# Attention's background work: order of the weight pieces, one bank for the block MLP, query splits one head at a time

## The chip, the core and the metric

The kernel runs on one core of one Trainium2 chip. The metric is the device time of one execution in microseconds (us); three runs of the kernel before gave a median of 1116.23 us (1115.17 to 1118.41). Times below are in us unless marked ns. PE is the tensor engine (PEld its weight load), DVE the vector engine, ACT the scalar engine, POOL GpSimd, and SP the engine whose queue issues most DMAs.

## The reference, cut to what matters

Two layers over 512 tokens of width 1024. The first is a short convolution with an MLP; then one shared key/value side is made; the second layer is native sparse attention with an MLP. The change touches only the attention.

```python
kv = (h @ w_kv).reshape(B, S, 6, 4, 64)            # 6 parts, 4 groups, 64 wide
k_raw, v_raw, k_sel, v_sel, k_win, v_win = (kv[:, :, i] for i in range(6))
k_cmp = compress_blocks(k_raw, cmp_pe_k, phi_k_w1, phi_k_w2)   # blocks of 32, stride 16 -> 31 tokens
v_cmp = compress_blocks(v_raw, cmp_pe_v, phi_v_w1, phi_v_w2)   # silu(flat @ w1) @ w2
q, gates = split(h2 @ w_qg)                        # 16 heads: 4 groups of 4
# per block of 128 queries, with a relative-position bias on all logits:
o = g0 * softmax(q k_cmp) v_cmp + g1 * softmax(q k_sel) v_sel + g2 * softmax(q k_win) v_win
x = x + o @ w_o
```

With 512 tokens the top-16 selection takes every causal block, and the window covers all tokens, so the selected and the windowed branch are both full causal attention with their own keys and values.

## The kernel before, in words

Every product of float32 values is made from float16 halves: a value is split into a high part `hi` and the remainder `lo`, and a product is three matmuls, hi x hi, hi x lo and lo x hi (`mm3`, L355 to L358). Weights come as 512 KB pieces in a fixed order (`pieces`, L74 to L132): `load_piece` issues the DMA on SP's queue (L150 to L173), with up to three pieces staged, `convert_piece` (L175 to L210) scales and splits one piece, on ACT (`whi`, L202) and DVE (`wlo`, L203), and `next_piece` (L213) hands the next one to its user, in the order of the list. `ahead_fine` (L707) converts up to two pieces ahead of use, 512 columns at a time, between the matmuls of whoever runs it.

Attention starts with a lead-in (L919): keys and values of the selected and windowed branches, queries of group 0, gates. Then comes a loop over 96 **items** (L1157). An item is one of

- `Full` (L971), 88 of them: logits of one group, one block of 128 queries and one branch against all earlier keys. An item has 512, 384, 256 or 128 columns a head, with one, two or four heads, so that it stays within 512 columns.
- `Cmp` (L1044), 8 of them: the compressed branch for two groups and one block of queries.

An item goes through five steps, which the loop hands out to different turns (`lead`, L1155). `st0`: logits on PE into PSUM bank tag "b" (two banks; L991 and L992, for `Cmp` L1061 and L1062), then DVE adds the bias and takes the row minimum (`at_s`, `at_m`, L999; three buffers of `at_s`), and ACT takes the exponential (`at_p`, L1001). `st1`, two turns later: PE transposes (bank "c", L1007), ACT takes the high half (`at_ph`, L1010). `st2`, three turns later: DVE takes the low half (`at_pl`, L1013). `st3`, four turns later: PE multiplies with the values (bank "d", L1026 to L1028; `Cmp` bank "e", L1098 to L1100); after the last head DVE scales by gate and row sum (`o_t`, L944), and POOL adds into `o` (L946, L949). `st4`, six turns later: PE transposes `o` (L960), and ACT and DVE split it into `big` (L377, L379), the operand of the output projection.

Beside the items runs a **background**, a chain of generators (L1140) that are pulled one step at a time. Each step tells its weight (0.65 for three matmuls of 512 columns, 0.42 for six of phi's of 155 columns); the loop adds a credit for each item (L1167: 1.03 up to item 43, then 0.78, 0.8 and 0.65) and pulls steps until the credit is used up. The parts stand one behind the other: `raw(0)`, `queries(1)`, `phi(0)`, `raw(1)`, `queries(2)`, `phi(1)`, `queries(3)`, then, once groups 0 and 1 are finished ("o1"), the output projection `out_proj(0)`. If an item needs something that is not yet done (`need`, L979 and L1050), the loop pulls the background until it is.

The background's parts, as far as the change touches them:

- `gated_pair` (L689): the projection of two 128-column blocks into two banks of tag "a" (there are two), in two pieces of weights. Used by `raw` and `queries`.
- `raw` (L786): the raw keys or values. DVE scales out of the "a" banks into `at_s` in another order of tokens (L797), ACT and DVE split it into `kr_hl` (one buffer; L377, L379), and twelve DMAs on SP's queue copy it into `big` (L803 to L805), the operand of phi.
- `phi` (L811): the block MLP. Four pieces of w1, each 24 matmuls of 155 columns from `big` into two banks of tag "a" (L823); then bias, tanh and split (L832 to L838, L381), and the second product into bank "e".
- `queries(g)` (L768): DVE scales the two "a" banks into `at_s` (L681), ACT copies each of the four heads to float16 (`Q`, L778, 64 partitions x 512), and POOL takes each remainder (L779). All four heads follow each other at once; three buffers of `Q`.

A scheduler places the instructions of each engine by their order in the source and by what they wait for; the order that results can be read from the built program.

## Time and profile before

| what | value |
|---|---|
| median of three runs | 1116.23 us (1115.17 to 1118.41) |
| the profiled execution | 1115.42 us |
| its span, first to last instruction | 1113.6 us |
| granted clock of PE | 0.998 of full |
| attention's items, first and last logits | about 549.8 and 757.0 us into the span |

The profile is of one execution. Its page gives the busy time of each engine, the chain of work that ended last, and the costliest groups; the trace behind it answers for single stretches and instructions. In a row "a<-b,c" is an instruction's output and inputs by their names in the program, "128x512" partitions by elements, and "[0.52 <-DVE at_s L797]" an idle time of the engine right before the instruction, with the instruction that ended it. "L797" is a line of the kernel before.

### The profile page before, as it was taken

What the parts mean: (1) busy time and instruction counts of PE and PEld (TensorE: products, weight loads), DVE (VectorE), ACT (ScalarE), POOL (GpSimd) and SP (SyncE); (2) the same over time, 40 slices, a digit from 0 to 9 for tenths busy, and PEclk for the clock granted to TensorE, in tenths of its full rate; (3) what the DMA queues carried; (4) which work ended last, traced back from release to release, by engine and by line L of the source; (5) the groups of instructions that cost most, each with busy time, mean ns of one, the idle gap of its engine ahead of it and who ended that gap; (6) DMA issues with size and microseconds to landing.
All of it is one profiled execution on the core that took longest, in us unless ns stands there. A gap on an engine that the chain in (4) does not pass through costs nothing.

```text
span 1113.6 us, 20039 instructions
## 1 busy us (share of the span) xinstructions
PE 1091.4 (98%) x7960; PEld 693.9 (62%) x7960; DVE 869.5 (78%) x1627; ACT 571.7 (51%) x922; POOL 58.5 (5%) x75
## 2 busy tenths in 40 slices
PE   9999999999999999999999999899999999999996
PEld 4444444446885448875767676675444788445895
DVE  5755466987988667969588889997998698875776
ACT  4532244545433444437578787875755433352352
POOL 1000000000000000000102021212000000000020
PEclk9999999999999999999999999999999999999999
DMA  6433335543333333303434242112653333330321
GB/s 214 132 97 95 114 95 151 152 119 108 114 115 115 99 109 99 111 18 119 122 98 132 66 128 63 39 40 64 184 158 106 98 118 108 114 95 1 96 77 76
DMA packets 149708, 115.74 MB, mean 104 GB/s; under 512 B 8700, under 2 KB 146640, under 8 KB 149616
## 3 DMA queue, kind: packets, MB, share of 16 engines
q1 hardware_dynamic: 146624, 108.88, 32.5%
q10 hardware_dynamic: 2608, 4.97, 1.5%
q8 instruction: 62, 1.02, 0.4%
q0 software_dynamic: 384, 0.63, 0.2%
q14 instruction: 30, 0.25, 0.1%
HBM read 110.22 MB, written 2.14 MB: 101 GB/s over the span
## 4 chain that ended last, share of the span: by engine, by line
PE 86%; DVE 7%; ACT 3%; issue 2%; POOL 1%; DMA 0%; DVEq 0%; ACTq 0%; SPq 0%
PE c L576 8%; PE a L576 8%; PE a L357 6%; PE a L356 6%; PE a L358 6%; PE b L576 6%; PE c L357 6%; PE c L358 6%; PE c L356 6%; PE b L358 6%; PE b L357 5%; PE b L356 5%; PE d L576 4%; PE e L576 2%; PE c L1007 2%
## 5 line engine op out<-in xcount | busy, mean ns | idle before, releaser
L202 ACT ACTIVATE whi<-wst 128x1024 f16<-128x1024 f32 (+3 forms) x172 | 144.3, 854 | 185.3 <-PE b L357 65.5
L203 DVE SCALAR_TENSOR_TENSOR wlo<-wst,whi 128x1024 f16<-128x1024 f32 (+3 forms) x172 | 170.1, 998 | 42.0 <-ACT whi L202 41.5
L576 PEld LDWEIGHTS <-whi 128*128 128x128 f16 x1792 | 175.3, 98 | 20.7
L358 PEld LDWEIGHTS <-wlo 128*128 128x128 f16 x1024 | 100.2, 98 | 111.7 <-DVE wlo L203 0.5
L356 PEld LDWEIGHTS <-whi 128*128 128x128 f16 x1024 | 100.3, 98 | 109.5 <-issue 2.5
L357 PEld LDWEIGHTS <-whi 128*128 128x128 f16 x1024 | 100.2, 98 | 108.4 <-issue 2.8
L189 ACT ACTIVATE whi<-wst 128x1792 f16<-128x1792 f32 x64 | 108.5, 1700 | 109.7 <-DVE wst L187 41.5
L190 DVE SCALAR_TENSOR_TENSOR wlo<-wst,whi 128x1792 f16<-128x1792 f32 x64 | 129.3, 2023 | 15.8 <-ACT whi L189 15.8
L187 DVE TENSOR_TENSOR wst<-wst 128x256 f32<-128x256 f32 x256 | 96.1, 428 | 19.6 <-DMA wst<-mlp_w_dram 18.3
L527 DVE TENSOR_TENSOR rl<-ml_z,rh 128x1792 f16<-128x1792 f32 x32 | 64.8, 2026 | 44.7 <-ACT rh L526 44.7
L576 PEld LDWEIGHTS <-wlo 128*128 128x128 f16 x896 | 87.7, 98 | 10.7 <-issue 0.2
L526 ACT ACTIVATE rh<-ml_z 128x1792 f16<-128x1792 f32 x32 | 54.3, 1696 | 57.3 <-DVE ml_z L525 57.3
L1001 ACT ACTIVATE at_p<-at_s,at_m 128x384 f32<-128x384 f32 (+3 forms) x128 | 70.8, 554 | 21.4 <-DVE at_m L999 20.5
L357 PE MATMUL b<-xsl,whi 128*128 128x512 f16 x208 | 78.9, 379 | 0.0
L358 PE MATMUL b<-xsh,wlo 128*128 128x512 f16 x208 | 78.9, 379 | 0.0
L356 PE MATMUL b<-xsh,whi 128*128 128x512 f16 x208 | 78.8, 379 | 0.0
L357 PE MATMUL c<-xsl,whi 128*128 128x512 f16 x192 | 72.8, 379 | 0.0
L356 PE MATMUL c<-xsh,whi 128*128 128x512 f16 x192 | 72.8, 379 | 0.0
L358 PE MATMUL c<-xsh,wlo 128*128 128x512 f16 x192 | 72.8, 379 | 0.0
L576 PE MATMUL c<-rh,whi 128*128 128x256 f16 x256 | 69.8, 273 | 0.0
L576 PE MATMUL c<-rl,whi 128*128 128x256 f16 x256 | 69.8, 273 | 0.0
L576 PE MATMUL c<-rh,wlo 128*128 128x256 f16 x256 | 69.8, 273 | 0.0
(318 smaller groups left out, 2549.9 us busy)
## 6 DMA issues: line engine op xcount, KB each, us to landing
wst<-mlp_w_dram SPq DMA_DIRECT2D x256, 256.0 KB, 3.4
wst<-a_w_in_dram SPq DMA_DIRECT2D x18, 512.0 KB, 3.6
wst<-w_kv_dram SPq DMA_DIRECT2D x12, 512.0 KB, 3.6
T<-ext_d ACTq DMA_DIRECT2D x4, 1056.0 KB, 6.1
wst<-a_w_out_dram SPq DMA_DIRECT2D x8, 512.0 KB, 3.5
wst<-b_w_qg_dram SPq DMA_DIRECT2D x8, 512.0 KB, 3.8
wst<-b_w_o_dram SPq DMA_DIRECT2D x8, 512.0 KB, 3.4
wst<-a_w_in_dram SPq DMA_DIRECT2D x7, 384.0 KB, 4.9
```

The lines of the kernel that those rows point to most:

```text
L187: DVE.tensor_tensor(b[:, :, o], b[:, :, x], b[:, :, y], op=e)
L189: ACT.activation(hi, b[:, :, 1:], AF.Copy, scale=sc)
L190: DVE.scalar_tensor_tensor(lo, b[:, :, 1:], sc, hi, op0=OP.mult, op1=OP.subtract)
L202: ACT.activation(hi[:, s:e], w, AF.Copy, scale=sc)
L203: DVE.scalar_tensor_tensor(lo[:, s:e], w, sc, hi[:, s:e], op0=OP.mult, op1=OP.subtract)
L356: PE.matmul(ps, w[0], xs[0], start=start, stop=False)
L357: PE.matmul(ps, w[0], xs[1], start=False, stop=False)
L358: return PE.matmul(ps, w[1], xs[0], start=False, stop=stop)
L526: ACT.activation(rh[0][:, p], z[:, 1:8], AF.Copy)
L527: DVE.tensor_tensor(rh[1][:, p], z[:, 1:8], rh[0][:, p], op=OP.subtract)
L576: PE.matmul(acc7[i], wl if n == 1 else wh, xl if n == 2 else xh, stop=c == 7 and n == 2, start=c == 0 and n == 0 and not other, skip_group ...
L1001: ACT.activation(self.p[:, w], lg[:, w], AF.Exp, bias=mn[:, j:j + 1], scale=-1.0, accum_out=l[:, br * 4 + h:br * 4 + h + 1])
```

## The change

- Pieces: the four pieces of phi_k_w1 and the two pieces of raw(1)'s weights (w_kv from column 256) now alternate: one, one, two, one, one.
- `phi` accumulates both halves in one bank, of tag "e" (columns 0 to 154 and 155 to 309), instead of two of tag "a"; only the first matmul of the first half opens the bank.
- The background runs `phi(0)` and `raw(1)` in turn, a step of each (`in_turn`).
- The generator that converts ahead is kept in one place (`fine`), and is finished before the next piece is handed out.
- `queries` scales into a tile of its own, `q_t`, instead of `at_s`. The four head splits go into a list (`later`), from which the loop takes one per item, or as many as an item needs. An item needs the last of its own heads ("q1.3"), not the whole group's.
- The compressed items of groups 0 and 1 stand behind the 4th, 6th, 8th and 10th item of group 2 (places 48, 51, 54, 57) instead of the 10th to 13th (54, 56, 58, 60).
- The credit is 1.17 up to item 46 and 0.65 after.

```diff
-    block(phi_k_w1, 0, SW, 0, 16)
+    for k in (0, 8):
+        block(phi_k_w1, 0, SW, k, 4)
+        cols(w_kv, 256, 256, SW, k // 2, 4)
+        block(phi_k_w1, 0, SW, k + 4, 4)
     cols(phi_k_w2, 0, 64, SW, 0, 2)
-    block(w_kv, 256)
...
         def ahead_fine():
-            while pos["cv"] < min(pos["use"] + AHEAD, len(pieces)):
-                yield from convert_piece(512)
+            drain(fine[0])
+            def convert():
+                while pos["cv"] < min(pos["use"] + AHEAD, len(pieces)):
+                    yield from convert_piece(512)
+            fine[0] = convert()
+            return fine[0]
...
             q = ap.tile([128, 4, S], F16, name="Q", bufs=3)
+            t = ap.tile([128, 2, S], F32, name="q_t", bufs=1)
+            Qs[g] = q
+            def head(h):
+                m, s = h // 2, h % 2
+                r, o = slice(64 * s, 64 * s + 64), slice(64 - 64 * s, 128 - 64 * s)
+                ACT.activation(q[r, h], t[r, m], AF.Copy)
+                POOL.tensor_tensor(q[o, h], t[r, m], q[r, h], op=OP.subtract)
+                done.add(f"q{g}.{h}")
             for m in range(2):
-                t = scaled(po[m], rbq)
-                for s in range(2):
-                    h, r = 2 * m + s, slice(64 * s, 64 * s + 64)
-                    o = slice(64 - 64 * s, 128 - 64 * s)
-                    ACT.activation(q[r, h], t[r], AF.Copy)
-                    POOL.tensor_tensor(q[o, h], t[r], q[r, h], op=OP.subtract)
-                yield
-            Qs[g] = q
+                DVE.tensor_tensor(t[:, m], po[m], rbq, op=OP.mult)
+            for h in range(4):
+                if lead_in[0]:
+                    head(h)
+                else:
+                    later.append(lambda h=h: head(h))
+            yield
...
-            ph = [bank("a"), bank("a")]
+            pb = bank("e")
+            ph = [pb[:, 0:155], pb[:, 155:310]]
...
-                        mm3(o, [...], rhs, cc == 0, cc == 15)
+                        mm3(o, [...], rhs, cc == 0 and m == 0, cc == 15, skip_group_check=m == 1)
...
+        def in_turn(*gens):
+            gens = list(gens)
+            while gens:
+                for k in list(gens):
+                    u = next(k, "end")
+                    if u == "end":
+                        gens.remove(k)
+                    else:
+                        yield u
...
-        items += mixed(full(2, (2, 3, 0, 1)), {9 + qb: Cmp(0, qb) for qb in range(4)})
+        items += mixed(full(2, (2, 3, 0, 1)), {3 + 2 * qb: Cmp(0, qb) for qb in range(4)})
...
             yield from raw(0)
-            yield from marked("q1", queries(1))
-            yield from phi(0)
-            yield from raw(1)
-            yield from marked("q2", queries(2))
+            yield from queries(1)
+            yield from in_turn(phi(0), raw(1))
+            yield from queries(2)
             yield from marked("cmp", phi(1))
-            yield from marked("q3", queries(3))
+            yield from queries(3)
...
                     while k not in done:
-                        if next(bg, "end") in ("wait", "end"):
+                        if later:
+                            later.pop(0)()
+                        elif next(bg, "end") in ("wait", "end"):
                             raise RuntimeError(k)
                 at_item.get(i, lambda: None)()
                 items[i].st0()
...
+                if later:
+                    later.pop(0)()
-            credit += 1.03 if i < 44 else 0.78 if i < 53 else 0.8 if i < 66 else 0.65
+            credit += 1.17 if i < 47 else 0.65
```

More of the change, by code (lines that the diff above doesn't have):

```diff
@@ L144, in body @@
     staged, ready = {}, {}
+    fine = [iter(())]
     pos = {"dma": 0, "cv": 0, "use": 0}
@@ L216, in next_piece @@
         pos["use"] += 1
+        drain(fine[0])
         while i not in ready:
-            for _ in convert_piece():
-                pass
+            drain(convert_piece())
         return ready.pop(i)
@@ L353, in rstd, with mm3 @@
             self.r = rstd_of(p[:, 0:4])
-    def mm3(ps, w, xs, start, stop):
-        PE.matmul(ps, w[0], xs[0], start=start, stop=False)
-        PE.matmul(ps, w[0], xs[1], start=False, stop=False)
-        return PE.matmul(ps, w[1], xs[0], start=False, stop=stop)
+    def mm3(ps, w, xs, start, stop, **k):
+        PE.matmul(ps, w[0], xs[0], start=start, stop=False, **k)
+        PE.matmul(ps, w[0], xs[1], start=False, stop=False, **k)
+        return PE.matmul(ps, w[1], xs[0], start=False, stop=stop, **k)
     def pair(xs, ps, kn=8, mid=None):
@@ L641, in body @@
         VC = ap.tile([128, 2, G, 4, 64], F16, name="VC")
-        Qs = {}
+        Qs, later = {}, []
         TG, TC = {}, {}
@@ L707, in ahead_fine @@
         def ahead_fine():
[L708 to L709 removed]
+            drain(fine[0])
+            def convert():
[3 more added lines that the diff above has]
+            return fine[0]
         def keys(br):
@@ L821, in phi @@
                     for m in range(2):
-                        o = ph[m][:, 0:155].rearrange("p (g j) -> p g j", g=5)
-                        mm3(o, [u[:, c, m * 128:(m + 1) * 128] for u in w], rhs, cc == 0, cc == 15)
+                        o = ph[m].rearrange("p (g j) -> p g j", g=5)
+                        mm3(o, [u[:, c, m * 128:(m + 1) * 128] for u in w], rhs, cc == 0 and m == 0, cc == 15,
+                            skip_group_check=m == 1)
                         next(cv, None)
@@ L917, in marked @@
             done.add(name)
-        for k in (keys(0), keys(1), marked("q0", queries(0)), values(0), values(1), gates()):
+        for k in (keys(0), keys(1), queries(0), values(0), values(1), gates()):
             drain(k)
@@ L979, in need @@
             def need(self):
-                return [f"q{self.g}"]
+                return [f"q{self.g}.{self.heads[-1]}"]
             def st0(self):
@@ L1050, in need @@
             def need(self):
-                return [f"q{2 * self.gp}", f"q{2 * self.gp + 1}", "cmp"]
+                return [f"q{2 * self.gp}.3", f"q{2 * self.gp + 1}.3", "cmp"]
             def st0(self):
```

## The prediction

> **What bounds the kernel now.** I read the page first, for which engine sets the end.
>
> ```profile
> span 1113.6 us, 20039 instructions
> PE 1091.4 (98%) x7960; PEld 693.9 (62%) x7960; DVE 869.5 (78%) x1627; ACT 571.7 (51%) x922; POOL 58.5 (5%) x75
> PE 86%; DVE 7%; ACT 3%; issue 2%; POOL 1%; DMA 0%; DVEq 0%; ACTq 0%; SPq 0%
> ```
>
> PE is busy for 98% of the span and carries 86% of the chain that ended last. The change touches only the attention stage, and the instructions of each engine are the same in kind and number before and after (in the built order, only their places differ, and the PSUM bank that phi writes). So all that it can win or lose is time in which PE waits. Next I cut the stage into stretches; columns are wall time, then busy time and count of PE, PEld, DVE, ACT, POOL. The first row is a stretch of MLP, for comparison.
>
> ```profile
> core 0: us, PE busy (x) PEld busy (x) DVE busy (x) ACT busy (x) POOL busy (x), PEclk, DMA share, GB/s
> 56.00:84.00 28.00, 28.00 (x131) 12.74 (x130) 15.71 (x22) 8.62 (x10) 0.00 (x0) 1.00 0.31 94
> 549.80:594.70 44.90, 43.62 (x428) 29.06 (x425) 34.60 (x97) 35.66 (x91) 4.34 (x5) 1.00 0.31 85
> 594.70:616.60 21.90, 19.50 (x244) 15.00 (x241) 20.04 (x62) 17.87 (x55) 3.54 (x4) 1.00 0.62 190
> 616.60:655.10 38.50, 37.85 (x408) 26.54 (x405) 31.32 (x93) 29.73 (x81) 4.68 (x6) 1.00 0.33 88
> 661.50:720.20 58.70, 54.32 (x666) 39.50 (x665) 56.54 (x175) 46.95 (x130) 14.59 (x17) 1.00 0.24 74
> ```
>
> PE never rests in the MLP; a 512-column matmul costs 28.00/131 = 0.214 there. In attention it loses 2.40 of 21.90 in the second stretch and 4.38 of 58.70 in the last. In that last one DVE is busy for 56.54 of 58.70: **there DVE is the limit**, and PE waits for it. Elsewhere both have room, so PE's waits must be collisions. Their rows (start, length, and in brackets the recorded idle with its releaser):
>
> ```profile
> 567.09 0.38 PE L356 MATMUL a<-xqh,whi 128*128 128x512 f16 x1 [0.52 <-DVE at_s L797]
> 590.81 0.23 PE L356 MATMUL a<-big,whi 128*128 128x155 f16 x1 [0.38 <-DVE at_s L681]
> 602.29 0.19 PE L1026 MATMUL d<-VT,at_ph 128*128 128x64 f16 x1 [0.68 <-DVE o_t L944]
> 605.67 0.52 PE L1007 MATMUL c<-ident,at_p 128*128 128x128 f32 x3 [0.59 <-DVE at_pl L1013]
> 607.26 0.32 PE L991 MATMUL b<-KD,Q 128*128 128x384 f16 x1 [0.39 <-DVE at_m L999]
> 608.33 0.32 PE L991 MATMUL b<-KD,Q 128*128 128x384 f16 x1 [0.53 <-DVE at_m L999]
> 609.03 0.52 PE L1007 MATMUL c<-ident,at_p 128*128 128x128 f32 x3 [0.21 <-DVE rl L1034]
> 629.64 0.38 PE L356 MATMUL a<-xqh,whi 128*128 128x512 f16 x1 [0.32 <-DVE at_s L797]
> 652.30 0.23 PE L356 MATMUL a<-big,whi 128*128 128x155 f16 x1 [0.33 <-DVE at_s L681]
> 656.12 0.34 PE L991 MATMUL b<-KD,Q 128*128 128x384 f16 x1 [0.29 <-POOL Q L779]
> 657.35 0.34 PE L991 MATMUL b<-KD,Q 128*128 128x384 f16 x1 [0.19 <-POOL Q L779]
> 703.10 0.63 PE L960 MATMUL c<-ident,o 128*128 128x128 f32 x4 [1.09 <-DVE at_pl L1013]
> 705.90 0.38 PE L356 MATMUL a<-big,whi 128*128 128x512 f16 x1 [1.45 <-ACT big L377]
> ```
>
> Two causes show. At 567, 590, 629 and 652 a background part starts, and its first matmul waits until DVE has emptied the two "a" banks of the part before. At 602 to 609, 656 and 703 PE waits for items' work that is late, each time behind a burst of four head splits:
>
> ```profile
> 590.91 2.57 ACT L778 ACTIVATE Q<-at_s 64x512 f16<-64x512 f32 x4
> 591.66 5.19 POOL L779 TENSOR_TENSOR Q<-at_s,Q 64x512 f16<-64x512 f32 x4 [8.81 <-ACT Q L778]
> 594.42 0.42 DVE L999 CUSTOM_DVE_ANT_0 at_s<-b,T 128x256 f32<-128x256 f32 x1 [0.94 <-POOL Q L779]
> DVE at_s L999 <- POOL Q L779: 3.3, 4, 1.2
> ```
>
> The burst takes ACT for 2.57 on end. POOL then holds two of the three at_s buffers for 5.19, so DVE, which needs one for an item's logits, stands still for 0.94 here and for 3.3 in four waits over the stage.
>
> A recorded idle is too small: the record of a matmul goes on after the next has started.
>
> ```profile
> 588.84 0.19 PE L1026 MATMUL d<-VT,at_ph 128*128 128x64 f16 x1
> 588.87 0.19 PE L1027 MATMUL d<-VT,at_ph 128*128 128x64 f16 x1
> 590.88 0.23 PE L357 MATMUL a<-big,whi 128*128 128x155 f16 x1
> ```
>
> Starts are 0.03 apart and records 0.19 long, so each stall costs PE 0.16 more than its bracket says; 155 columns cost 0.07 (590.81 to 590.88). In the same way a 512-wide DVE instruction costs about 0.60, not its record's 0.68:
>
> ```profile
> 578.08 0.68 DVE L999 CUSTOM_DVE_ANT_0 at_s<-b,T 128x512 f32<-128x512 f32 x1
> 578.69 0.08 DVE L999 DVE_READ_ACCUMULATOR2_ANT at_m<- 128x1 f32 x1
> L797 DVE TENSOR_TENSOR at_s<-a,rb 128x512 f32<-128x512 f32 x4 | 3.9, 1020 | 0.0
> L999 DVE CUSTOM_DVE_ANT_0 at_s<-b,T 128x128 f32<-128x128 f32 x32 | 7.4, 287 | 0.4 <-PE b L992 0.3
> ```
>
> **The change part by part.**
>
> *A, stalls that go.* phi now writes bank "e", so phi(0) and phi(1) no longer wait for the queries' eviction: 590.81 (0.38) and 652.30 (0.33) go. The queries are scaled into a tile of their own and split one head per item, so ACT's 2.57 becomes four blocks of about 0.64, one per item, and no at_s buffer is held: 656.12 and 657.35 (0.29 + 0.19) go. In 602 to 609 (0.68 + 0.59 + 0.39 + 0.53 + 0.21 = 2.40) there is a third reason: phi(0) has ended, and raw(1) cannot begin before its "a" banks are evicted, so PE has nothing between the items. Now raw(1) runs in turn with phi(0), and in the built order each item from 15 to 29 has a fill of 9 matmuls or more. Recorded sum 0.71 + 0.48 + 2.40 = 3.59; with 0.16 for each of nine stalls **5.0**. If half of the 602 to 609 group stays, 3.4; nothing there can cost more than before unless DVE runs late, which is a rival.
>
> *B, a stall that grows.* phi(0) and raw(1) now end in the same item, 29, and the next part, queries(2), needs the "a" banks. DVE must do, after the logits of item 30, four 128-wide at_s (4 x 0.21), two small phi and positional instructions (about 0.4) and L797 twice (each 1.02 less the 0.08 overlap): the first bank is free 2.7 after PE's first logits of item 30 (half a microsecond of lag counted in), the second 3.6. PE has 2.0 of work of its own until then (in items 30 to 32, in proportion to columns: logits three times 0.43, three transposes at 0.11, eleven 64-column matmuls at 0.03). It waits 0.7, does three matmuls (0.64), and waits 0.3 more: 1.0, where 629.64 cost 0.32 + 0.16 = 0.5. DVE may come to it late by a conversion and a memset (1.2 more). I take **+0.8** (0.5 to 1.7). The 567.09 stall stays as it is.
>
> *C, the DVE-bound stretch.* Compressed items come at places 48, 51, 54, 57 instead of 54, 56, 58, 60, and the filler runs faster (1.17 per item, was 1.03). I counted both built orders from the logits of item 48 to those of item 76. PE has 10.4 less to do there: 9 fewer groups of three 512-column matmuls (9 x 0.642 = 5.8), 48 fewer of phi's (48 x 0.07 = 3.4), 42 fewer of 64 columns (1.2). That work stands earlier, where DVE and ACT had room. DVE's own work from item 48 to 74 is 42 instructions of 512 columns (42 x 0.60 = 25.3) and narrower ones for 18.4: 43.7, where before it was 52.5 (phi(1)'s tail and seven conversions have moved ahead). Before, PE took 60.4 from item 48's first logits to item 76's (1.7 ahead of the 58.70 of the row above). After: 0.6 until DVE has the logits, 43.7, DVE's idle time, and 2.3 from DVE's item 74 to PE's item 76. Idle was 58.70 - 56.54 = 2.2, over half of it behind the splits of q3, which goes:
>
> ```profile
> 705.33 0.42 DVE L999 CUSTOM_DVE_ANT_0 at_s<-b,T 128x256 f32<-128x256 f32 x1 [1.24 <-POOL Q L779]
> ```
>
> But with thinner fill DVE will more often wait for ACT and PE. I take 2.0 (1 to 4), thus 48.6. Wall falls by 11.8, fill of 10.4 is paid elsewhere: **-1.4** (-2.4 to +0.6). The 703.10 and 705.90 stalls lie inside this sum: the output projection still starts right behind the last transposes of groups 0 and 1, and its operand still comes by ACT's L377, now without four query splits ahead of it.
>
> *D, the rest.* The pieces' order on SP's queue puts two of w_kv between those of phi_k_w1; loads are as many and as large, each still three pieces ahead of its use, and raw(1)'s twelve copies into "big" stand between them as before. phi(0) starts three items earlier, about 584 to 586, behind copies that take their data when raw(0) is evicted, as before; I cost it at 0, hidden by queries(1), and 1 if that cover fails. The conversions' order follows the pieces; the same number falls to ACT and DVE. The added wait on a single head ("q1.3") has nothing queued behind it, since splits are written out before the item that needs them.
>
> One thing speaks against spreading the splits. A DVE instruction beside POOL's split was slower than elsewhere:
>
> ```profile
> 574.09 0.16 DVE L1034 TENSOR_TENSOR rl<-rl,GT 128x8 f32<-128x8 f32 x1
> 595.12 0.53 DVE L1034 TENSOR_TENSOR rl<-rl,GT 128x8 f32<-128x8 f32 x1
> ```
>
> That is 0.37 for one meeting. Four meetings in the DVE-bound stretch cost up to 1.5; the burst had some of them already. I take **+0.4** (0 to 1.5). The Trainium skill, page "SBUF — State Buffer", section "Who interferes with whom", says that a VectorE instruction with two SBUF inputs and a GpSimd instruction that reads SBUF shut each other out for the whole instruction; by this the price of a meeting is the rest of the POOL instruction rather than a share. The row at 595.12 is in line with a wait of part of one split.
>
> Sum: -5.0 + 0.8 - 1.4 + 0.4 = -5.2. The profiled execution took 1115.42 (span 1113.6 and 1.8 around it), so 1110.2; it lies 0.8 below the median of the runs, 1116.23, and on that footing the forecast is **1111.0**.
>
> **The rivals.**
>
> *Given back.* PE's work is the same in all, and fill that is used early is missing late. If A is only 3.4, B is 1.7 and C is +0.6, the sum is -0.7: about 1115.5. For it speaks that DVE is busy 96% of the DVE-bound stretch already; against it that DVE loses 8.8 of work there, only 1.6 less than the fill that PE loses.
>
> *Locked out.* Each of q3's four splits shuts DVE out for its full length, 5.19/4 = 1.3: 5.2 instead of 0.4, and the sum is -0.4: 1115.8. The row at 595.12 speaks against full length. This is the page's rule at its strictest.
>
> *Starved: slower.* In items 48 to 64 PE has few filler groups left, and each item is a chain through PE, DVE, ACT and back. If DVE has to wait for its turn in that chain, its idle time becomes wall time one for one. With A and B at -4.2 net, the gain is gone when C is +4.2, which is 2.0 + 5.6 = 7.6 of DVE idle in that stretch, against 2.2 before. At 13 of idle (half a microsecond for each of 26 items) the sum is -4.2 + 9.6 + 0.4 = +5.8: 1122. Against it: four items are in flight between the first and the last step, and with the same four DVE's waits for ACT within an item were few and short:
>
> ```profile
> DVE at_pl L1013 <- ACT at_ph L1010: 8.3, 13, 1.4
> ```
>
> That is 8.3 in 13 waits over the whole attention stage, none above 1.4.
>
> *Not as named.* phi(0) and raw(1) would not run in turn if raw's weights came late; the built order shows them in turn, and the pieces stand in the order of use. I give it no chance of its own.
>
> **How the numbers follow.** Forecast, 1107 to 1112.8: 0.54. Better than that, with DVE idle near 1 and no lock-out: 0.08. Given back or locked out, 1113 to 1118: 0.25. Starved, above 1119: 0.13. A measurement of this kernel can tell about 0.3%, 3.3, from no change, so below 1112.9 is faster: 0.62; within: 0.25; slower: 0.13. The range 1106.5 to 1118.5 leaves out part of the second case (0.06) and the slower one (0.13).
>
> **What would show it.** A is right if no row of PE near 585 to 612 has an idle time of over 0.3 with releaser at_s, at_pl or POOL Q, and if no wait of DVE for POOL Q is left. B is right if the largest idle time of PE between 600 and 640 stands before the first xqh matmul of queries(2), released by L797, at 0.8 or so recorded. C is right if PE reaches the 28 items' end about 4 sooner than at 720.2, and DVE idles 1 to 4 between items 48 and 74. The forecast is wrong if DVE's busy share from items 48 to 64 falls below 85%, if transposes of items wait there for exponentials, or if L203 and L1034 grow beside POOL's splits.

## The result, and the profile after

The changed kernel takes **1119.42** us (median of 22 runs, 1117.57 to 1121.86) where the kernel before takes 1116.27 (22 runs): a ratio of 1.0027, 95% interval 1.0021 to 1.0033. It is slower by 3.2, and the forecast was 1111.0, faster by 5.2. The profiled execution of after spans 1116.8, against 1113.6 before: the same 3.2. (Lines of after stand 4 to 31 further down: L356 to L358 are now L360 to L362, L797 is L816, L1007 is L1038, L1013 is L1044, L203 is L207, L1034 is L1065, L778 and L779 are L789 and L790.)

The page of after, first lines and the shares of the chain:

```profile
span 1116.8 us, 20032 instructions
PE 1092.0 (98%) x7960; PEld 693.2 (62%) x7960; DVE 870.2 (78%) x1627; ACT 572.0 (51%) x922; POOL 57.4 (5%) x75
PE 84%; DVE 7%; ACT 6%; issue 2%; DMA 1%; POOL 0%; ACTq 0%; DVEq 0%
```

Each engine has as many instructions as before. In the chain ACT has 6% where it had 3%, and DMA 1% where it had 0%. The stretches of attention, now cut by items. First before, from the first logits of item 16 to those of item 28 and from there to item 48; then after, the same two and those to items 66 and 76 (columns as in the prediction's table):

```profile
585.50:609.70 24.20, 21.42 (x298) 18.03 (x294) 21.12 (x62) 21.30 (x58) 5.70 (x5) 1.00 0.42 124
609.70:659.80 50.10, 48.97 (x535) 34.57 (x532) 41.20 (x120) 38.48 (x108) 7.54 (x8) 1.00 0.32 92
```

```profile
587.40:618.50 31.10, 27.78 (x337) 21.34 (x333) 24.25 (x66) 22.18 (x58) 6.08 (x6) 1.00 0.41 120
618.50:674.40 55.90, 52.98 (x610) 37.84 (x607) 49.97 (x139) 44.72 (x130) 7.74 (x9) 1.00 0.37 108
674.40:704.40 30.00, 26.16 (x323) 18.92 (x322) 28.11 (x88) 23.97 (x60) 10.79 (x11) 1.00 0.07 20
704.40:724.30 19.90, 19.73 (x250) 14.77 (x247) 19.55 (x67) 16.69 (x54) 2.44 (x4) 1.00 0.16 47
```

The filler has moved ahead as the built order said: 535 matmuls in items 28 to 48 are now 610. In the first of after's rows PE stands 3.3 of 31.1, in the second 2.9 of 55.9; before it was 2.8 of 24.2 and 1.1 of 50.1. So the loss is not in the DVE-bound stretch that I feared (third and fourth row), but ahead of it.

Recorded idle is too small, so for all kernels I took the starts of successive matmuls and subtracted what each width takes when PE runs without a break (512 columns 0.216, 384 0.162, 256 0.109, 155 0.070, 128 0.056, 64 0.029, a float32 transpose 0.109). What is left is time in which PE stands. By stage, in us, with the median times (the stages are those of the profiled execution, which lies within 0.9 of the median in most kernels, but 1.0 below it in rate_only_added, 1.7 below in skew_rate_early, 1.1 above in heads_only and 2.2 above in late_spread):

| kernel | items 0-16 | 16-28 | 28-48 | 48-76 | 76-94 | sum | time |
|---|---|---|---|---|---|---|---|
| before | 1.4 | 4.0 | 2.0 | 7.7 | 1.2 | 16.3 | 1116.3 |
| after | 1.4 | 3.8 | 4.8 | 7.7 | 1.7 | 19.3 | 1119.4 |

The sums differ by 3.0, nearly all of the 3.2. In the same account the rest of the kernel agrees to 0.2 between the two, but for the first and last 56 us, which vary by 0.4 to 0.5. The rows of PE behind it, in the timeline of after (the waits over 0.5 recorded, from item 16 to the output projection):

```profile
589.80 0.63 PE L1038 MATMUL c<-ident,at_p 128*128 128x128 f32 x4 [0.79 <-DVE at_pl L1044]
606.74 0.63 PE L1038 MATMUL c<-ident,at_p 128*128 128x128 f32 x4 [0.56 <-DVE at_pl L1044]
616.36 0.19 PE L1057 MATMUL d<-VT,at_ph 128*128 128x64 f16 x1 [1.98 <-DVE o_t L975]
625.89 0.38 PE L360 MATMUL a<-xqh,whi 128*128 128x512 f16 x1 [0.76 <-DVE at_s L816]
660.20 0.19 PE L1057 MATMUL d<-VT,at_ph 128*128 128x64 f16 x1 [0.56 <-DVE o_t L975]
669.79 0.20 PE L886 MATMUL e<-whi,kr_hl 128*128 128x64 f16 x1 [0.79 <-DVE kr_hl L881]
692.34 0.66 PE L1038 MATMUL c<-ident,at_p 128*128 128x128 f32 x4 [0.99 <-DVE big L383]
697.29 0.63 PE L991 MATMUL c<-ident,o 128*128 128x128 f32 x4 [0.76 <-DVE at_pl L1120]
702.68 0.66 PE L1038 MATMUL c<-ident,at_p 128*128 128x128 f32 x4 [0.60 <-DVE at_pl L1044]
```

None of the nine stalls of part A is among them, and over the whole stage no wait of PE is released any more by L685 (L681 before) or by POOL's Q. But three others stand in items 16 to 28, and the largest, at 616.36, is one that the forecast had nowhere. Its cause can be read back from engine to engine in the same timeline:

```profile
604.67 0.37 ACTq L659 DMA_DIRECT2D T<-ext_d  x1
606.02 0.37 SPq L175 DMA_DIRECT2D wst<-b_w_qg_dram  x1
613.39 1.06 ACT L206 ACTIVATE whi<-wst 128x1024 f16<-128x1024 f32 x1 [1.68 <-DMA wst<-b_w_qg_dram]
614.36 0.60 ACT L1032 ACTIVATE at_p<-at_s,at_m 128x384 f32<-128x384 f32 x1
614.48 1.23 DVE L207 SCALAR_TENSOR_TENSOR wlo<-wst,whi 128x1024 f16<-128x1024 f32 x1 [1.54 <-ACT whi L206]
615.62 0.68 DVE L975 TENSOR_TENSOR o_t<-d,rl 128x512 f32<-128x512 f32 x1
```

The second weight piece of queries(2) is issued at 606.02, behind the third bias table (1056 KB, 604.67). ACT stands in the piece's conversion for 1.68 until it lands; an item's exponential is queued behind the conversion. DVE stands in the other half of the conversion for 1.54, and the scaling at L975 is queued behind that, for which PE waits with bank "d".

### The profile page after: what moved, and what is told of

Its sections match the earlier page's. It is cut to its first block, busy times and chain, and to the rows that moved or that the text cites. A ratio compares the mean times of both kernels' runs of the same rounds, so it can differ in the third digit from the quotient of the medians.

```text
span 1116.8 us, 20032 instructions
## 1 busy us (share of the span) xinstructions
PE 1092.0 (98%) x7960; PEld 693.2 (62%) x7960; DVE 870.2 (78%) x1627; ACT 572.0 (51%) x922; POOL 57.4 (5%) x75
## 3 DMA queue, kind: packets, MB, share of 16 engines
HBM read 110.22 MB, written 2.14 MB: 101 GB/s over the span
## 4 chain that ended last, share of the span: by engine, by line
PE 84%; DVE 7%; ACT 6%; issue 2%; DMA 1%; POOL 0%; ACTq 0%; DVEq 0%
PE a L580 8%; PE c L580 7%; PE a L361 6%; PE a L360 6%; PE a L362 6%; PE b L580 6%; PE c L362 6%; PE c L360 6%; PE c L361 6%; PE b L362 5%; PE b L361 5%; PE b L360 5%; PE d L580 4%; PE e L580 2%; PE c L1038 1%
## 5 line engine op out<-in xcount | busy, mean ns | idle before, releaser
L207 DVE SCALAR_TENSOR_TENSOR wlo<-wst,whi 128x1024 f16<-128x1024 f32 (+3 forms) x172 | 170.6, 1001 | 44.7 <-ACT whi L206 44.6
L362 PEld LDWEIGHTS <-wlo 128*128 128x128 f16 x1024 | 100.2, 98 | 111.8 <-DVE wlo L207 0.7
L360 PEld LDWEIGHTS <-whi 128*128 128x128 f16 x1024 | 100.2, 98 | 110.5 <-issue 2.5
L191 DVE TENSOR_TENSOR wst<-wst 128x256 f32<-128x256 f32 x256 | 94.8, 418 | 19.8 <-DMA wst<-mlp_w_dram 18.5
L362 PE MATMUL b<-xsh,wlo 128*128 128x512 f16 x208 | 78.8, 379 | 0.0
L360 PE MATMUL b<-xsh,whi 128*128 128x512 f16 x208 | 78.7, 379 | 0.0
L360 PE MATMUL c<-xsh,whi 128*128 128x512 f16 x192 | 72.8, 379 | 0.0
L362 PE MATMUL c<-xsh,wlo 128*128 128x512 f16 x192 | 72.8, 379 | 0.0
```

The lines of the kernel that those rows point to most:

```text
L191: DVE.tensor_tensor(b[:, :, o], b[:, :, x], b[:, :, y], op=e)
L207: DVE.scalar_tensor_tensor(lo[:, s:e], w, sc, hi[:, s:e], op0=OP.mult, op1=OP.subtract)
L360: PE.matmul(ps, w[0], xs[0], start=start, stop=False, **k)
L362: return PE.matmul(ps, w[1], xs[0], start=False, stop=stop, **k)
```

## The experiments

All times are medians, with the ratio to the kernel before on the same chip and its 95% interval. The theory after reading the trace, "late weight": the loss comes from phi(0) in turn with raw(1), above all through that late piece. Its rival, "thin fill": filler used early is missing later, so places and rate cost.

**Parts alone.** Each of the first four kernels is before with some hunks of the change: phi's bank; the splits; places and rate; bank and in turn.

```diff
-            ph = [bank("a"), bank("a")]
+            pb = bank("e")
+            ph = [pb[:, 0:155], pb[:, 155:310]]
```

> The kernel before with one edit: phi accumulates in one "e" bank instead of two "a" banks. All theories: the two waits of phi's first matmul for the queries' eviction (0.38 and 0.33 recorded, 0.16 more each) go, so 1.0 us less than before (0.5 to 1.5). If instead the queries' eviction is waited for later by raw(1) or queries(3), the gain is under 0.3.

Measured 1117.58, ratio 1.0014 (1.0005 to 1.0023): slower, where 1.0 less was expected. PE's standing falls by 1.0 up to item 36, as said, and rises by 2.3 in items 48 to 76. The timeline of this kernel shows where:

```profile
702.15 2.58 ACT L778 ACTIVATE Q<-at_s 64x512 f16<-64x512 f32 x4
702.91 4.83 POOL L779 TENSOR_TENSOR Q<-at_s,Q 64x512 f16<-64x512 f32 x4 [3.70 <-issue]
705.32 0.42 DVE L1001 CUSTOM_DVE_ANT_0 at_s<-b,T 128x256 f32<-128x256 f32 x1 [1.89 <-POOL Q L779]
706.93 0.44 PE L993 MATMUL b<-KD,Q 128*128 128x384 f16 x1 [2.80 <-DVE at_m L1001]
```

The last group's burst of splits still holds two at_s buffers. It now catches DVE for 1.89 (before 1.24), and PE, whose logits follow DVE's, for 2.80. A wait removed in one place came back at the next holder of the same buffers.

```diff
+            t = ap.tile([128, 2, S], F32, name="q_t", bufs=1)
...
+                    later.append(lambda h=h: head(h))
```

> The kernel before with the queries scaled into a tile of their own and split one head per item, nothing else. Both theories: DVE's 3.3 us of waits for POOL's splits go and the PE stalls at 656 and 657 with them: 1 to 2 us less than before. If a split beside DVE's work locks DVE out for its whole length, the gain is under 0.3 or the time is longer.

Measured 1115.01, 0.9994 (0.9985 to 1.0003): not to be told from no change. By stage its profiled execution loses 0.9 ahead of item 16 and 1.1 from there to 48, and gains 1.5 from 48 to 76.

```diff
-        items += mixed(full(2, (2, 3, 0, 1)), {9 + qb: Cmp(0, qb) for qb in range(4)})
+        items += mixed(full(2, (2, 3, 0, 1)), {3 + 2 * qb: Cmp(0, qb) for qb in range(4)})
...
-            credit += 1.03 if i < 44 else 0.78 if i < 53 else 0.8 if i < 66 else 0.65
+            credit += 1.17 if i < 47 else 0.65
```

> The kernel before with the compressed items at places 48, 51, 54, 57 and the faster filler (1.17 per item to item 46, then 0.65), nothing else. Theory 'late weight' (the loss comes from phi(0) and raw(1) in turn): 0 to 1.5 us less than before. Theory 'thin fill' (the fill used early is missing from item 48 on): 2 to 4 us more than before.

Measured 1119.82, 1.0034 (1.0021 to 1.0046): alone they cost as much as the whole change. But of the 3.5 that PE stands longer (19.8 against 16.3), 3.1 lie between items 28 and 48, 0.5 after item 76, and nothing from 48 to 76: the time is that of "thin fill", the place is not.

```diff
-            yield from phi(0)
-            yield from raw(1)
+            yield from in_turn(phi(0), raw(1))
```

(with the bank, and the pieces in the order of the change)

> The kernel before with phi in the "e" bank and phi(0) in turn with raw(1) (pieces in that order), old splits, places and filler rate. Theory 'late weight': the second weight piece of queries(2) is loaded late, ACT stands in its conversion, and the time is 1 to 3 us above the run with the "e" bank alone. Theory 'thin fill': in turn is good by itself, 2 to 2.5 us below the run with the "e" bank alone.

Measured 1118.31, 1.0016 (1.0008 to 1.0025): 0.7 above the bank alone, which can't be told from nothing, and between the theories. In turn does save in items 16 to 28 (1.8 against 2.8 for the bank alone), and gives it back in 28 to 48 (3.2 against 2.0) and in 48 to 76 (1.1 more).

**Parts together.** The changed kernel without new places and rate (both lines below); with the new rate and the old places (the first line only); and the bank and the splits alone, phi(0) ahead of raw(1) and the pieces as before.

```diff
-        items += mixed(full(2, (2, 3, 0, 1)), {3 + 2 * qb: Cmp(0, qb) for qb in range(4)})
+        items += mixed(full(2, (2, 3, 0, 1)), {9 + qb: Cmp(0, qb) for qb in range(4)})
...
-            credit += 1.17 if i < 47 else 0.65
+            credit += 1.03 if i < 44 else 0.78 if i < 53 else 0.8 if i < 66 else 0.65
```

> The changed kernel without two of its parts: compressed items at the old places (54, 56, 58, 60) and the old filler rate; "e" bank, one split per item and in turn stay. Theory 'places' (the places and rate cost 3 to 4 us, the rest gains 1 to 3): 1113 to 1115.5. Theory 'late weight' (phi(0) in turn with raw(1) costs 2 by itself, through the second weight piece of queries(2)): 1117 or more.

> The changed kernel with the compressed items at the old places, but with the new filler rate. If the faster filler alone makes the loss (fill gone before the compressed items come): 1118 to 1121, at or above the changed kernel. If the places make it: as the kernel without both, 1113 to 1115.5.

> The kernel before with the "e" bank and one split per item; phi(0) ahead of raw(1) as before, old places and rate. The stalls at 602 to 609 (2.4 recorded) stay, so by my first reasoning 1.5 to 2.5 us above the kernel that has in turn as well; by theory 'late weight' 1 to 2 us below that.

Measured 1116.05, 1.0000 (0.9991 to 1.0010); 1118.89, 1.0022 (1.0013 to 1.0031); and 1114.17, 0.9979 (0.9970 to 0.9988). So neither theory has it alone. The faster rate costs 2.8, the places on top of it 0.5, which can't be told from nothing. In turn costs 1.9, against my expectation of a gain of 2. And bank and splits together gain 2.2, though one alone loses 1.4 and the other's gain is unresolved: the splits take the at_s buffers out of the way that made the bank alone slow.

| kernel | items 0-16 | 16-28 | 28-48 | 48-76 | 76-94 | sum | time |
|---|---|---|---|---|---|---|---|
| bank and splits (no_in_turn) | 1.7 | 2.4 | 2.1 | 7.9 | 1.2 | 15.1 | 1114.2 |
| and in turn (all_but_places) | 1.8 | 1.4 | 4.2 | 8.1 | 1.2 | 16.6 | 1116.1 |
| and the rate (rate_only_added) | 1.5 | 3.0 | 4.6 | 7.9 | 1.3 | 18.4 | 1118.9 |

In turn gives 1.0 in items 16 to 28, where part A had counted on 3.2 from it, and costs 2.1 in 28 to 48. The rate costs 1.6 in 16 to 28. Along this chain of kernels, from before to after, the steps are -2.2 (bank and splits), +1.9 (in turn), +2.8 (rate) and +0.5 (places).

**The late piece.** The table's load can't be issued much earlier, since its buffer is the first table's; it can be issued later.

```diff
-        at_item = {11: lambda: load_T(1), 35: lambda: load_T(2), 60: lambda: load_T(3)}
+        at_item = {11: lambda: load_T(1), 22: lambda: load_T(2), 60: lambda: load_T(3)}
```

> The changed kernel, with the load of the third bias table (1056 KB) issued at item 22 instead of 35, so that it no longer runs beside the load of the second weight piece of queries(2). If that load's 7.4 us are the table's doing, ACT's wait of 1.7 and PE's stall of 2.1 at 614 go: 1117.0 to 1118 us against 1119.4. If the piece is late because it is issued late, the stall stays and the time is unchanged within 0.7.

Measured 1117.75, 1.0008 (0.9999 to 1.0016): 1.7 less than after. The load moved by only 1.9, to 602.8, but that took it off the piece: PE stands 1.0 instead of 3.8 in items 16 to 28. Another wait of ACT came up instead, 1.73 up to 633.05 for the copies into `big`, and behind it one of PE of 1.68 recorded.

```diff
-        at_item = {11: lambda: load_T(1), 35: lambda: load_T(2), 60: lambda: load_T(3)}
+        at_item = {11: lambda: load_T(1), 31: lambda: load_T(2, items[29].exp), 60: lambda: load_T(3)}
...
+            with tc.issue_after(behind.ins) if behind else nullcontext():
```

> The changed kernel with the load of the third bias table held back behind item 29's exponential (about 621 us, was issued at 604.7). Theory 'load collision': the second weight piece of queries(2) lands about 4 us after its issue instead of 7.4, ACT's wait of 1.7 and PE's 2.1 at 614 go; 1116.5 to 1118 us. If the piece is late by its own issue time alone: 1119.4 within 0.7.

Measured 1116.98, 1.0005 (0.9997 to 1.0014): 2.4 less than after. The time from issue to landing of the weight pieces issued between 596 and 632, first in after (where the late piece took 7.3, and the one issued behind it 7.4), then here:

```profile
DMA to landing us min/median/max: 3.8/4.0/7.4
```

```profile
606.57 0.37 SPq L175 DMA_DIRECT2D wst<-b_w_qg_dram  x1
611.70 1.06 ACT L206 ACTIVATE whi<-wst 128x1024 f16<-128x1024 f32 x1 [0.47 <-PE e L361]
DMA to landing us min/median/max: 3.6/3.9/4.5
```

The piece is issued no earlier, 606.57, yet it takes 3.6 and no load over 4.5, and ACT starts its conversion at 611.70 without waiting for a DMA. PE's 2.14 is gone (no wait of PE is recorded from 612 to 617.5). So the late piece is settled: the table beside it made the load 7.3 long.

**The end of phi(0) and raw(1).** In the kernel with in turn at the old rate, PE waits 0.71 and 1.29 before queries(2):

```profile
626.69 0.19 PE L1057 MATMUL d<-VT,at_ph 128*128 128x64 f16 x1 [0.71 <-DVE o_t L975]
628.14 1.95 DVE L816 TENSOR_TENSOR at_s<-a,rb 128x512 f32<-128x512 f32 x2
629.20 0.38 PE L360 MATMUL a<-xqh,whi 128*128 128x512 f16 x1 [1.29 <-DVE at_s L816]
```

DVE empties the two banks only at 628.14, after phi's tanh chain, which it shares with ACT (the last matmul into those banks ended at 623.99). With phi a quarter ahead (the pieces in that order too) the chain is over sooner:

```diff
-            yield from in_turn(phi(0), raw(1))
+            p = phi(0)
+            for _ in range(4):
+                yield next(p)
+            yield from in_turn(p, raw(1))
```

> The kernel without new places and rate (1116.05), with phi(0) one quarter ahead of raw(1) instead of beside it, so that phi's exponential chain on DVE and ACT is over when raw(1)'s two 'a' banks have to be emptied. Theory 'coincident ends' (PE's stall before queries(2), 1.46 and 0.87 there, comes of both parts ending together): stall under 0.6, 1113.8 to 1115 us. If the stall is that of the 'a' banks alone, as before phi's end is beside the point: 1116 within 0.6.

```profile
625.60 0.63 PE L1038 MATMUL c<-ident,at_p 128*128 128x128 f32 x4 [0.52 <-DVE rl L1065]
626.90 1.01 DVE L816 TENSOR_TENSOR at_s<-a,rb 128x512 f32<-128x512 f32 x1
627.71 0.22 PE L360 MATMUL e<-phi_h,phi_w 128*128 128x128 f16 x1 [0.37 <-ACT phi_h L381]
```

Measured **1113.86**, 0.9980 (0.9971 to 0.9989): 2.2 less, and the wait before the xqh matmul is gone. The bank is free at 627.9, and PE has phi's second product in between.

**Both mended.** The table held back at the old rate, and the whole change with phi ahead and the table held back:

> phi(0) a quarter ahead, old places and rate, and the table held back. The table costs nothing here by the traces (no wait of ACT for a weight piece at the old rate), so the same as the run with phi(0) ahead alone within 0.7; if the table's transfer disturbs anything else, 1 us lower.

> The whole changed kernel with both suspects mended: phi(0) a quarter ahead, and the third table held back. If the late load and the coincident ends are what the forecast missed, the gain of part A shows: 1113.5 to 1115.5 us. If the faster filler costs by itself from item 44 on (thin fill), it stays at 1117 or more.

Measured 1114.92, 0.9990 (0.9981 to 0.9998), and 1116.76, 1.0002 (0.9993 to 1.0011). The first is a miss: where there was no collision, holding the table back seems to cost 1.1 (the intervals overlap; by stage it is 1.3 in items 28 to 48). The second lies between what the two expectations said: with both mended the new places and rate still cost 1.8 (the intervals overlap a little). By stage that is 0.9 in items 16 to 28, where PE waits 1.35 for o_t at 606.01, and 0.5 after item 76; with 0.2 less from 48 to 76 they make 1.1 of the 1.8. Two comparisons limit what phi's lead is worth. Against the kernel with the table held back alone (1116.98) it gains 0.2 here, which can't be told from nothing: its 2.2 show at the old rate only. And at the old rate it stands at 1113.86, where the bank and the splits without in turn have 1114.17: the lead repays what in turn costs, and no gain beyond that can be told.

| kernel | items 0-16 | 16-28 | 28-48 | 48-76 | 76-94 | sum | time |
|---|---|---|---|---|---|---|---|
| table_late | 2.1 | 1.8 | 4.6 | 7.7 | 1.7 | 17.8 | 1117.0 |
| phi_ahead | 1.7 | 1.0 | 2.9 | 8.0 | 1.2 | 14.8 | 1113.9 |
| phi_ahead_table_late | 1.4 | 1.0 | 4.2 | 7.9 | 1.2 | 15.7 | 1114.9 |
| both_mended | 1.4 | 1.9 | 4.2 | 7.7 | 1.6 | 16.8 | 1116.8 |

**The rate, early or late.** phi ahead, and 1.17 up to item 43 only:

```diff
-            credit += 1.03 if i < 44 else 0.78 if i < 53 else 0.8 if i < 66 else 0.65
+            credit += 1.17 if i < 44 else 0.78 if i < 53 else 0.8 if i < 66 else 0.65
```

> phi(0) a quarter ahead, old places, and the filler rate of 1.17 up to item 43, then as before (0.78, 0.8, 0.65). If the early rate costs (fill used up where the items could spare it, loads earlier against the table's transfer): 1115.5 to 1117. If the late part of the new rate (0.65 from item 47) made the cost: 1113.5 to 1114.5.

Measured 1122.14, 1.0059 (1.0046 to 1.0073): 8.3 above phi ahead. So the early part of the rate costs, and more than I had thought. It is also 3.3 above the kernel with the whole new rate at the old places (1118.89), so the slower late part may repay some of it; that kernel has no lead of phi, so this is not shown. PE stands 6.1 in items 28 to 48 and 9.8 from 48 to 76.

**The splits.** They do not come one per item. Of the second group, ACT does one at 586.52 and three on end at 588.35, and of the fourth group four on end, in the timeline of after:

```profile
586.80 2.25 DVE L207 SCALAR_TENSOR_TENSOR wlo<-wst,whi 128x512 f16<-128x512 f32 x2
587.28 1.23 POOL L790 TENSOR_TENSOR Q<-q_t,Q 64x512 f16<-64x512 f32 x1 [2.89 <-ACT Q L789]
588.35 1.93 ACT L789 ACTIVATE Q<-q_t 64x512 f16<-64x512 f32 x3
588.98 0.68 DVE L1044 SCALAR_TENSOR_TENSOR at_pl<-c,at_ph 128x512 f16<-128x512 f32 x1
...
652.29 2.39 POOL L790 TENSOR_TENSOR Q<-q_t,Q 64x512 f16<-64x512 f32 x2 [2.64 <-ACT Q L789]
653.56 1.28 DVE L207 SCALAR_TENSOR_TENSOR wlo<-wst,whi 128x128 f16<-128x128 f32 x1
...
668.67 0.72 POOL L977 TENSOR_TENSOR o<-o_t 128x256 f32<-128x256 f32 x1 [7.65 <-DVE o_t L975]
668.70 1.23 DVE L881 COPY kr_hl<-phi_h 128x512 f16<-128x512 f16 x2
...
696.43 2.57 ACT L789 ACTIVATE Q<-q_t 64x512 f16<-64x512 f32 x4
```

For comparison, the conversions from 596 to 660 by form (shortest, median and longest in ns), and two copies that stand alone:

```profile
L207 DVE SCALAR_TENSOR_TENSOR wlo<-wst,whi x19: 279/686/1276, 595.5 to 656.9; 128x512 f16<-128x512 f32 x16, 128x128 f16<-128x128 f32 x2, 128x1024 f16<-128x1024 f32 x1
666.74 0.49 DVE L881 COPY kr_hl<-phi_h 128x512 f16<-128x512 f16 x2
```

They also show DVE shut out. The two conversions at 586.80 take 2.25, where two take 1.29 alone (below); at_pl, for which PE waits at 589.80, comes 0.96 late. The 128x128 conversion at 653.56 takes 1.28, where the other one of its kind takes 0.28: it ends 0.16 after POOL's second split (652.29 and 2.39). The two copies at 668.70 take 1.23 beside an addition of POOL's, and 0.49 at 666.74. Two theories, bursts on ACT or shut-out by POOL, were put to four runs. The first, on table_late, forces one split per item; the second does the same on phi ahead; the third, on table_late, lets POOL write zeros:

```diff
-                ACT.activation(q[r, h], t[r, m], AF.Copy)
+                with tc.issue_after(behind.ins) if behind else nullcontext():
+                    ACT.activation(q[r, h], t[r, m], AF.Copy)
...
-                    later.pop(0)()
+                    later.pop(0)(items[i].exp)
```

> The changed kernel with the table held back (1116.98), and each split of the queries held behind another item's exponential, so that they do come one per item. Theory 'bursts' (three and four splits on end on ACT delay the items' chain at 588 and 696): PE's stalls at 588.7 (0.96) and 696 to 702 (2.7 in four) shrink by half or more, 1114.5 to 1116 us. Theory 'lock-out' (what hurts is that GpSimd's splits keep DVE's conversions out): spread splits meet more of DVE's work, 1117 to 1118.5.

> The fastest so far (phi(0) a quarter ahead, old places and rate, 1113.86) with the splits forced apart in the same way. Theory 'bursts': 1112 to 1113.3. Theory 'lock-out': 1114 to 1115.5.

```diff
-                POOL.tensor_tensor(q[o, h], t[r, m], q[r, h], op=OP.subtract)
+                POOL.memset(q[o, h], 0.0)
```

> The changed kernel with the table held back, in which GpSimd sets the low halves of the queries to zero instead of computing them (so it leaves out the low part of the logits), and reads no SBUF for it. Theory 'lock-out': the conversion at 587 takes 0.69 instead of 1.65, PE's stall at 588.7 goes, 1115.5 to 1116.3 us against 1116.98. Theory 'bursts': ACT's three splits on end stay and with them the stall, 1117 within 0.5.

Measured 1118.14, 1.0023 (1.0013 to 1.0033); 1114.55, 0.9988 (0.9979 to 0.9997); 1116.52, 1.0006 (0.9997 to 1.0015). Spreading by itself is no gain: 1.2 more than table_late, where the intervals just overlap, and 0.7 more than phi ahead, where they overlap widely. In the third the conversions are back at 1.29 for two, and the wait at 589 is gone, in the timeline of that kernel:

```profile
585.50 2.24 POOL L791 MEMSET Q<- 64x512 f16 x4
587.86 1.29 DVE L207 SCALAR_TENSOR_TENSOR wlo<-wst,whi 128x512 f16<-128x512 f32 x2
```

The zeros come earlier than the splits did and meet no conversion, so this shows what the meeting had cost there, not that a write alone does no harm. ACT still does its splits one and then three on end (587.57 and 589.40), so that stall was not the burst's. The time fell by 0.5 only, as "bursts" had it, less than the intervals tell: PE waits elsewhere instead, so that items 16 to 28 stand 1.7, as against 1.8 in table_late.

By stage, spreading with phi ahead gains 0.7 in items 16 to 28 (and 0.3 before them) and 1.4 in 48 to 76 (1.2 from 48 on), and loses 2.7 in between. There the third group's items follow at once, and wait for the splits themselves, in the timeline of skew_spread:

```profile
655.05 0.34 PE L1023 MATMUL b<-KD,Q 128*128 128x384 f16 x1 [0.77 <-POOL Q L791]
658.28 1.43 DVE L207 SCALAR_TENSOR_TENSOR wlo<-wst,whi 128x512 f16<-128x512 f32 x1 [0.94 <-ACT whi L206]
659.22 0.34 PE L1023 MATMUL b<-KD,Q 128*128 128x384 f16 x1 [0.78 <-POOL Q L791]
```

So the last run spreads the splits of the second and fourth groups only:

```diff
-                    later.append(lambda b, h=h: head(h, b))
+                    later.append(lambda b, h=h: head(h, b if g != 2 else None))
```

> phi(0) a quarter ahead, old places and rate, with the splits of the second and fourth groups held one per item and those of the third as they fall. If the account by stages adds up (lock-out beside conversions in the third group's splits, bursts in the others): 1113.86 - 0.7 - 1.4 = 1111.8 us (1111.2 to 1113). If the stages aren't independent (the fourth group's gain came of reaching it later): 1113.5 to 1114.5.

Measured **1112.56**, 0.9969 (0.9959 to 0.9980): the fastest of all, 3.8 below the kernel before and 6.9 below the changed one (and 1.3 below phi ahead, where the intervals just overlap). It keeps the "e" bank, the splits from their own tile and in turn, with phi a quarter ahead, and has the old places and rate.

| kernel | items 0-16 | 16-28 | 28-48 | 48-76 | 76-94 | sum | time |
|---|---|---|---|---|---|---|---|
| late_spread | 1.9 | 1.3 | 3.6 | 9.9 | 1.7 | 18.3 | 1118.1 |
| skew_spread | 1.4 | 0.3 | 5.6 | 6.6 | 1.4 | 15.3 | 1114.6 |
| spread_q1_q3 | 1.4 | 0.3 | 2.9 | 7.5 | 1.2 | 13.3 | 1112.6 |

The stages are nearly independent: 0.3 and 2.9 are as the two parents have them; of the 1.4 expected from item 48 on, 0.5 came.

## Why the prediction was wrong

By stage the forecast said -3.7 (A) for items 16 to 28, -1.3 (A) and +0.8 (B) for 28 to 48, -1.4 (C) and +0.4 (D) from 48 on. Measured in PE's standing: -0.2 and +2.8, and from 48 on -0.1 and, after item 76, +0.5. So the miss is about 3.5, 3.3 and 1.4.

**The step that failed first is D's sentence on the loads**, "loads are as many and as large, each still three pieces ahead of its use". It put the new order of the pieces at nothing: no term of the sum stands for it. (The 0 in the same paragraph is for phi(0)'s earlier start, and no wait of PE for those copies is recorded in after.) The sentence is true of the count and says nothing of the time. Three pieces ahead are issued when a staging buffer is free, and with the pieces used two at a time the second piece of queries(2) came 7.6 behind the first, at 606.02, where in the timeline of before both were issued ahead of the table (the last row gives landing times, for the pieces issued from 585 to 632):

```profile
597.89 4.14 SPq L171 DMA_DIRECT2D wst<-b_w_qg_dram  x2
602.76 0.37 ACTq L655 DMA_DIRECT2D T<-ext_d  x1
604.52 16.11 SPq L171 DMA_DIRECT2D wst<-phi_v_w_dram  x4
DMA to landing us min/median/max: 3.8/3.9/7.9
```

(The second of the two ends its issue at 602.03.) The table made loads slow before the change, too: the two pieces of phi_v issued behind it, at 604.52 and 606.81, took 7.9 and 7.2, but no conversion waited for them. So the change brought a piece that is soon due into a place where a load is slow. I had looked at SP's queue and not at the table on ACT's. The step measured 2.4 (after against table_late), 2.0 of it in items 16 to 28, where 3.7 of A's 5.0 should have shown.

**A was right in its rows and wrong in its sum.** All nine stalls are gone; so is DVE's wait for POOL's splits. But its sign, no idle over 0.3 for at_pl near 585 to 612, was not met: 589.80 and 606.74 stand there. Without the collision most of the first stage's gain shows: with the early table, items 16 to 28 stand 1.0 instead of 4.0. With the collision and the new rate away and phi ahead they stand 1.0 as well, but the 1.3 of items 28 to 48 does not come (2.9 against 2.0 before), and the time falls by 2.2. And "four blocks of about 0.64, one per item" was false: in the timeline of after the splits stand one and three, two and two, and four on end. Forcing them apart was no gain by itself.

**B was right as a stall, and more stands beside it.** The waits before queries(2)'s first two matmuls of the banks are 0.76 and 0.13 recorded, with 0.16 for each 1.2, against 0.5 at 629.64: +0.7, forecast +0.8. By its sign it should have been the largest wait of PE between 600 and 640, and that is the one at 616.36. B had the two parts end in one item, but it had no price for the items that DVE then makes late: at 624.54 PE waits 0.43 recorded for an item's at_m. Items 28 to 40 stand 1.85 longer than before (2.49 against 0.64), above the 1.7 of B's upper end. At the old rate the same place cost more (1.29 recorded, and 0.71 ahead of it), and phi ahead took 2.2 off the time there.

**C was right in mechanism, and its value was nothing.** In the DVE-bound stretch, from 674.40 to 704.40, DVE is busy 28.11 of 30.00, so "Starved" did not come about: I had set 85% for that, and it is 94%. The wall from item 48 to 76 is 49.9 (674.4 to 724.3), forecast 48.6, which is within its range; but the wall falls by 10.5 and the fill of 10.4 is paid elsewhere, so the gain is 0.1, not 1.4. DVE's idle time was as its sign said (busy 44.5 of 46.8 from item 48 to 74), but PE reaches the 28 items' end at 724.3, 4 later than 720.2 and not 4 sooner. What I priced as free, paying that fill earlier, was not: the rate costs 2.8, by stage 2.0 of it in items 16 to 48. Some of that is the collision (PE waits 1.12 for o_t at 616.14 in rate_only_added, as it does at 616.36 in after), but 1.8 are left, with the places, after both are mended. That the early part costs by itself is shown by the run with 1.17 up to item 43; by which chain, in items 28 to 48, stays open.

**D's lock-out was too small where it mattered.** I took 0.4 for four meetings in the DVE-bound stretch. The longer meetings came earlier: on DVE 0.96 at 586.80, 1.00 at 653.56, and one of another kind at 668.70, where two copies took 1.23 instead of 0.49. PE waits behind the first, at 589.80, and behind the third, at 669.79. The Trainium skill, page "SBUF — State Buffer", section "Who interferes with whom", calls the lock between such instructions exclusive. The 128x128 conversion bears it out: it takes 1.28 instead of 0.28 and ends 0.16 after POOL's split. So the prediction's own sign, L203 growing beside POOL's splits, came true. The 0.37 that I took for a share may have been a meeting that began late in the split.

The rival "Given back" came nearest in kind, 1115.5 forecast, as fill used early was paid for; the one on the slower side, "Starved" at 1122, had the sign and not the place. Of the missed cases, a load that lands late stood nowhere in the sum, and two parts that end at once stood in B without the items that wait beside them. Both mended, the whole change still takes 1116.76, so they make 2.7 of the 8.4 between forecast and measurement; what keeps A's gain from showing at the new rate stays open beyond that.

## What to carry to other kernels

"As many pieces ahead as before" is a count: look up at what time the load is issued after the change, what else is in transfer then on every queue, and which engine stands in the conversion with work queued behind it. Two parts run in turn had better not end together: a quarter's lead was worth 2.2 here at the old rate, though at the new one nothing that could be told. And a stall removed is only worth its time if the buffers' next holder isn't worse: the bank alone lost 1.4, the two together gained 2.2.

## What the runs showed that I had not expected

A weight load of 512 KB that took about 4 away from the table's load took 7.3 beside it (1056 KB, issued 1.35 before), and held up PE by 2.14 through two other engines. A copy of float16 from SBUF to SBUF on DVE was slowed beside a GpSimd addition of 0.72, much as the conversions with two inputs are (two took 1.23, alone 0.49). And forcing ACT's splits apart, which looks like the more even schedule, did not help where all groups were spread (1.2 and 0.7 slower), and seems to help, by 1.3 with intervals that just overlap, where the group that is needed at once was left alone.
